# Two-bank output parts, plain transposes, one prefix sum a pair, and ScalarE's own DMA queue in a two-layer decoder trunk

## The chip, the cores and the metric

The kernel runs on one core of one Trainium2 chip. Such a core has five engines with one instruction stream each: TensorE (PE in the rows; its weight loads are PEld), VectorE (DVE), ScalarE (ACT), GpSimd (POOL) and SyncE (SP), which issues DMAs. ScalarE can issue DMAs as well. Matrix products land in PSUM, which has eight banks; everything else is held in SBUF. The metric is the device time of one execution in microseconds. A granted clock of 1.00 for TensorE means 2.4 GHz, 0.50 means 1.2 GHz.

## What is computed

The reference is a decoder of two layers over 1024 positions with a width of 1024. Layer 0 mixes positions with a gated linear recurrence (Hawk), layer 1 with a delta-rule state of 64x64 per head and 16 heads (RWKV-7). A SwiGLU feed-forward and a gated embedding product follow each. The change is inside the second mixer, whose core is this recurrence:

```python
def step(S, inp):
    r_t, w_t, k_t, v_t, a_t, b_t = inp
    sa = jnp.einsum('bhvk,bhk->bhv', S, a_t)
    S = S * w_t[:, :, None, :] + sa[..., None] * b_t[:, :, None, :] + v_t[..., None] * k_t[:, :, None, :]
    y = jnp.einsum('bhvk,bhk->bhv', S, r_t)
    return S, y
```

Around it stand projections for r, k, v, small low-rank products for the decay w, for a and for the gate g, a normalisation of k per head, and after it a normalisation of y per head, a bonus term, the gate and an output projection.

## The kernel before, in words

The 1024 positions are worked in two halves of 512, called t = 0 and 1. The width of 1024 is eight tiles of 128 rows (index j), and a tile of 128 rows holds two heads of 64. All dense products use a split of each operand into a high and a low part and three matmuls (`mm3`), with 512 columns. Their weights come by DMA in pieces of 128x512 into `raw` (two buffers while the recurrence runs), ScalarE rounds them into the high part (L239), GpSimd forms the low part (L240), and the pair stands in `whl` (four buffers). One piece serves 12 dense matmuls.

The recurrence is done in chunks of 64 positions, eight per half, by four generators in `scan()`:

- `stage1` goes over 16 pairs (half, tile). `prep` loads a, w, k and q, forms the running sum of w inside each chunk with eight scans of 64 columns (L1004), and exponentials of it. Products of these give BK and ZL; two groups of eight matmuls (`sc`) give the within-chunk products, which DVE masks out of PSUM (L1070 to L1072). A group of 16 matmuls (`bkt`, L1090) multiplies BK with a diagonal matrix `dg` of the chunk's total decays PC, which GpSimd builds (L1034); that is a transpose with scaling. ScalarE copies it out, and it is stored in DRAM (`bk`).
- `inverse` inverts the triangular matrices of two pairs at a time, with DVE work and five groups of small matmuls (w, n, u, w, v), and stores them (`inv`).
- `stage2` runs over the 16 chunks in order and carries the state SV. Per chunk: 16 matmuls `zu<-SV,ZC`, a copy to z, 16 matmuls `zu<-z,VC`, a copy to SU (ScalarE and DVE), 16 matmuls `zu<-SU,BC` whose result DVE adds to `ss` (the old state times PC, formed ahead at L1229) for the new state, and 32 matmuls into `y` (L1253, L1254): for each of 16 head slots one from SV and one from SU, accumulating in the same PSUM place. ScalarE copies y out.
- `norm2` normalises y per head and pair of tiles, with two matmuls `bsum` and two `yv` for each pair of tiles.

Which matmul follows which on TensorE is written out by a small planner. While the generators live, TensorE's instructions keep their program order (`manual_schedule`). The dense code calls `tick()` after each matmul, and a generator's next piece is put there when the planner's own clock has passed the piece's due time and when enough PSUM tiles of the ring `b` are free by its count. That ring has `BANKS` tiles; a piece that yields 2 wants two. `until()` moves the planner's clock on when no dense work is to be put in. The other engines are ordered by priorities, where `ahead(n)` moves code n places forward.

Stores of finished tiles to DRAM are issued on SP's queue, in one order with the loads of the weights. The names in the rows are those of the tiles; L116 is the helper `mm` by which all matmuls are recorded, and an fp32 matmul leaves two records in the trace.

Of the kernel before, what the change touches and what calls it, by code (L numbers as in the profile page):

```python
# [24 lines left out]

BANKS = 3
PACE = ((3, 1200), (2.5, 200))
LEAD_O, LEAD_F, LEAD_E, LEAD_P = 2, 2, 1, 2  # L30
IN = 2
# [28 lines left out]
class Kern:  # L60
# [680 lines left out]
    def rwkv_proj(self, t):  # L741
# [39 lines left out]
        def lora2(nm, bias, hs, n0, n1):  # L781
            w2 = []

            def item(n):
                if not w2:
                    w2.append(self.load_w(A["lora2_" + nm][:, n0 * 128 : n1 * 128], (n1 - n0) * 128))
                ps = self.ps("lx")
                a = (n - n0) * 128, (n - n0) * 128 + 128
                self.mm(ps, w2[0](0, *a), hs, True, False)
                self.mm(ps, w2[0](1, *a)[0:64], hs[0:64], False, True)  # L790
                self.tick()
                o = self.t2("o")
                with self.aux():
                    self.sigmoid(o, ps, self.v(bias, n), self.nb[bias][:, n : n + 1])
                nc.sync.dma_start(self.act_d[nm, n, t], o)
                self.done.add((nm, n, t))

            return [lambda n=n: item(n) for n in range(n0, n1)]
# [18 lines left out]
        def gate2(gh, gl, gs, q):  # L817
            w = []

            def item(n):  # L820
                if not w:
                    for nm in ("lora2_g", "lora2_gb"):
                        w.append(self.load_w(A[nm][:, q * 512 : q * 512 + 512], 512))
                    nc.vector.tensor_copy(w[1](0, 0, 512)[64:96], w[1](1, 0, 512)[64:96].bitcast(F32))
                a = n * 128, n * 128 + 128
                ps = self.ps("gx")
                self.mm(ps, w[0](0, *a), gh, True, False)
                self.mm(ps, w[0](0, *a), gl, False, False)
                self.mm(ps, w[0](1, *a), gh, False, False)
                self.mm(ps, w[1](0, *a)[:96], gs[:96], False, True)  # L830
                self.tick()
                o = self.t2("o")
                with self.aux():
                    nc.scalar.copy(o, ps)
                nc.sync.dma_start(self.act_d["g", 4 * q + n, t], o)
                self.done.add(("g", 4 * q + n, t))

            return [lambda n=n: item(n) for n in range(4)]
# [19 lines left out]
        def proj(i, j, nm, ext=None, xs=None, mid=None, n0=4):  # L858
            if xs is None:
                xs = self.rwkv_mix(xn, j, ext)  # L860
                self.pause(PM)

            def after(n, o, f):
                if f is not None:
                    f()
                if nm == "v":
                    ps = self.ps("vtr").rearrange("p (c k) -> p c k", c=4)
                    for c in range(4):
                        self.mm(ps[:, c, :], o[:, c * 128 : c * 128 + 128], self.cst[:, 128:256])
                    z = self.t2("vt").rearrange("p (h c k) -> p h c k", c=4, k=64)  # L870
                    with self.aux():
                        nc.scalar.copy(z, ps.rearrange("p c (h k) -> p h c k", k=64))
                    x = self.vt_d[t][:, :, :, n, :].rearrange("s h (c e) k -> e s h c k", e=2)
                    for e in range(2):
                        nc.sync.dma_start(x[e], z[e * 64 : e * 64 + 64])
                self.done.add((nm, n, t))

            for ns in self.lead([*range(KD)], LEAD_P):
                if mid is not None and n0 in ns:
                    mid()  # L880
                qs = []
                for n in ns:
                    if len(ns) > 1:
                        qs.append((self.ps("pps"), self.halves(A["rkv"][i, n], None, xs, t)))
                    else:
                        w = self.load_w(A["rkv"][i, n], 1024)
                        qs.append((self.ps("pps"), self.wx(w, KD, xs, t)))
                self.mm3(*qs)
                self.flush()
                for n, (ps, _) in zip(ns, qs):  # L890
                    o = self.t2("o")
                    with self.aux():
                        if n % 2:
                            nc.scalar.copy(o, ps)
                        else:
                            nc.vector.tensor_copy(o, ps)
                    nc.sync.dma_start(self.act_d[nm, n, t], o)
                    f = unit(n, o) if nm == "k" else None
                    self.later.append(lambda n=n, o=o, f=f: after(n, o, f))
            if not self.region:  # L900
                self.flush()
# [20 lines left out]
    def scan_begin(self, sp, pp):  # L922
        nc, A = self.nc, self.A
        self.sp, self.spp = sp, pp
        self.zu = pp.tile([128, KD, 64], F32, name="zu")
        self.yp = pp.tile([128, KD, 64], F32, name="y")
        self.Pp = sp.tile([128, NC, 65], F32, name="Pp")
        nc.vector.memset(self.Pp[:, :, 0:1], 1.0)
        self.D16 = sp.tile([128, 32, 16], F32, name="D16")
# [9 lines left out]
    def scan(self):  # L939
# [55 lines left out]
        def stage1():  # L995
            Pp = self.Pp

            def prep(t, j):
                at = ld("a", j, t)
                sw = ld("w", j, t)  # L1000
                kt = ld("k", j, t)
                L = tt("L")
                for c in range(0, TH, 64):
                    nc.vector.tensor_tensor_scan(  # L1004
                        L[:, c : c + 64], self.ones[:, 0:64], sw[:, c : c + 64], 0.0, ALU.mult, ALU.add)
                nc.scalar.activation(Pp[:, :, 1:65], c3(L), AF.Exp, scale=-C0)
                nc.scalar.activation(L, L, AF.Exp, scale=C0)
                return at, kt, L, ld("q", j, t), sw
# [2 lines left out]
            for P, (t, g, jj) in enumerate(order):  # L1011
# [17 lines left out]
                    PCs[t] = sp.tile([128, NC, KD], F32, tag="PC", name="PC", bufs=2)  # L1029
                PC = PCs[t][:, :, j]  # L1030
                nc.vector.tensor_copy(PC, Pp[:, :, 64])

                dg = sp.tile([128, NC, 64], F32, tag="dg", name="dg", bufs=1)
                nc.gpsimd.tensor_mul(dg, ident.unsqueeze(1).to_broadcast([128, NC, 64]), PC.unsqueeze(2).to_broadcast([128, NC, 64]))  # L1034

                old = (P - 3) // 2
                yield 4000, False, (lambda: old < 0 or inv[old] >= 2)
# [49 lines left out]
                pss = [c3(big("bkt", e)) for e in (500, 900)]  # L1087
                for c in range(NC):
                    for hh, me, ot in HV:
                        self.mm(pss[hh][:, c, :], BK[me, c, :, :].rearrange("p i s -> p (i s)"), dg[me, c, :])  # L1090
                        self.clock -= 77
                evac()
                evac()
                with self.ahead(AHEAD_S1):
                    for hh in range(2):
                        nc.scalar.copy(BKt[:, :, hh, :], pss[hh])
                nc.sync.dma_start(self.bk_d[t][:, :, j, :], BKt.rearrange("p c h k -> p c (h k)"))
                s1[G] += 10
                if nxt is not None:
                    yield 1000, False, None  # L1100
# [1 line left out]
        def inverse():  # L1102
# [16 lines left out]
            for G in range(NG):  # L1119
# [54 lines left out]
                with ahead():  # L1174
                    for p0 in (0, 64):
                        nc.scalar.copy(V[p0 : p0 + 32, :, :, 32:64], ps[p0 : p0 + 32].rearrange("p (j c) k -> p j c k", j=2))
                nc.sync.dma_start(self.inv_d[G // 4][:, :, 2 * (G % 4) : 2 * (G % 4) + 2, :], Vt)
                yield 1000, False, None
                inv[G] = 3

        def stage2():
# [3 lines left out]
            def state():  # L1185
                return sp.tile([128, 2, KD, 64], F32, tag="SV", name="SV", bufs=2)
# [21 lines left out]
            for t in range(2):  # L1208
# [4 lines left out]
                for c in range(NC):  # L1213
# [6 lines left out]
                    for j in range(KD):  # L1220
                        for hh, me, ot in HV:
                            self.mm(ps[me, j, :], ZL[:, j, hh * 128 : hh * 128 + 64], SV[:, hh, j, :])
                    self.clock = at + 650
                    with ahead():
                        nc.scalar.copy(z, ps)
                        if upd:
                            ss = sp.tile([128, KD, 64], F32, tag="ss", name="ss", bufs=1)
                            for hh, me, ot in HV:
                                nc.vector.tensor_mul(ss[me], SV[me, hh], PC[me, c, :].unsqueeze(2).to_broadcast([64, KD, 64]))  # L1229
                            SVn = state()  # L1230
                        if c < NC - 1:
                            nxt = load(t, c + 1, SVn)
                    yield ZLAT, False, None
                    at = self.clock
                    for j in range(KD):
# [8 lines left out]
                    if upd:  # L1244
                        for j in range(KD):
                            for hh, me, ot in HV:
                                self.mm(ps[me, j, :], BKc[:, j, hh * 64 : hh * 64 + 64], SU[:, hh, j, :])
                        with ahead():
                            for hh, me, ot in HV:
                                nc.vector.tensor_add(SVn[me, hh], ps[me], ss[me])  # L1250
                    for j in range(KD):
                        for hh, me, ot in HV:
                            self.mm(yp[me, j, :], SV[:, hh, j, :], ZL[:, j, hh * 128 + 64 : hh * 128 + 128], True, False)  # L1253
                            self.mm(yp[me, j, :], SU[me, hh, j, :], ZL[me, j, 256:320], False, True)  # L1254
                    self.clock = at + 2000
                    if c % 2 == 0:
                        ys = sp.tile([128, KD, 2, 64], F32, tag="yc", name="yc", bufs=1)
                    with ahead():
                        nc.scalar.copy(ys[:, :, c % 2, :], yp)
                    if c % 2:  # L1260
                        nc.sync.dma_start(self.y_d[t][:, :, c * 64 - 64 : c * 64 + 64], ys.rearrange("p j c k -> p j (c k)"))
                    if upd:
# [226 lines left out]
```

## Time and profile before

| | us |
|---|---|
| median of 3 runs | 3225.04 (3216.24 to 3226.09) |
| profiled execution | 3224.65 |
| its span | 3222.9 |
| PE, PEld busy | 3038.5, 2386.2 |
| DVE, ACT, POOL busy | 1618.0, 1359.2, 1301.1 |

The span runs from the first to the last instruction of the profiled execution. Busy times count an engine's instructions; a wait is put down to what came last before it ended. The kernel moves 415.20 MB by DMA, 129 GB/s on average, nearly all of it through one queue issued from SP.

### The profile page before, as it was taken

Reading aid. Unit: us, or ns where it says so; the run is one execution under the profiler, and the core shown is the slowest. Engines: PE = TensorE matmul, PEld = TensorE weight load, DVE = VectorE, ACT = ScalarE, POOL = GpSimd, SP = SyncE. Lnnn points to the kernel's source line nnn. Section 1 sums busy time; section 2 is a strip of 40 time slices with the busy share of each in tenths; the row PEclk is TensorE's granted clock in tenths of the full one; section 3 lists DMA queues with packets and bytes.
Section 4 is the critical chain, followed back from the end, with each engine's and each line's share of the span. In section 5 each row is a group of like instructions: output and inputs, shape, how many; then the busy total and the mean of one; then the engine's idle time right before and its main releaser. Section 6 shows DMA issues by size and latency. Waiting matters only on the chain. (4 is left out here: it accounts for less than half of the span.)

```text
span 3222.9 us, 45692 instructions
## 1 busy us (share of the span) xinstructions
PE 3038.5 (94%) x17160; PEld 2386.2 (74%) x17160; DVE 1618.0 (50%) x2498; ACT 1359.2 (42%) x2213; POOL 1301.1 (40%) x1082
## 2 busy tenths in 40 slices
PE   5999999999999889999999878888999999999998
PEld 4777778887867667777777556667777777888886
DVE  8765751222572467773336556688322356312145
ACT  5574742323565334334344752333322345422244
POOL 5111144444554445444223354443322345544445
PEclk9999999999999989999888998889988899999999
DMA  3111133332336464444443676544444363333323
GB/s 126 59 43 45 51 98 95 95 95 92 119 118 211 155 207 159 156 146 135 151 155 107 221 231 187 174 139 155 134 135 153 105 220 104 105 95 95 95 84 106
DMA packets 269148, 415.20 MB, mean 129 GB/s; under 512 B 40704, under 2 KB 108032, under 8 KB 266880
## 3 DMA queue, kind: packets, MB, share of 16 engines
q1 hardware_dynamic: 268640, 411.93, 39.9%
q8 instruction: 135, 2.21, 0.3%
q14 instruction: 85, 0.70, 0.1%
q10 hardware_dynamic: 288, 0.37, 0.0%
HBM read 319.92 MB, written 92.27 MB: 128 GB/s over the span
## 5 line engine op out<-in xcount | busy, mean ns | idle before, releaser
L240 POOL TENSOR_TENSOR whl<-raw,whl 128x512 fp32r<-128x512 f32 (+2 forms) x818 | 1052.4, 1292 | 1511.6 <-ACT whl L239 1458.2
L239 ACT CAST whl<-raw 128x512 fp32r<-128x512 f32 (+2 forms) x818 | 482.6, 593 | 927.2 <-PE ops L116 249.4
L116 PE MATMUL pg<-xn,whl 128*128 128x512 f32 (+1 forms) x2184 | 524.5, 394 | 7.0 <-ACT xn L290 4.8
L116 PE MATMUL ops<-hid,whl 128*128 128x512 f32 x2112 | 513.1, 400 | 19.0 <-ACT hid L290 7.2
L116 PEld LDWEIGHTS ops<-hid,whl 128*128 128x128 f32 x2112 | 400.8, 192 | 119.6 <-DVE hid L291 14.3
L116 PEld LDWEIGHTS pg<-xn,whl 128*128 128x128 f32 x2184 | 408.1, 189 | 101.9 <-ACT xn L290 6.7
L116 PE MATMUL pu<-xn,whl 128*128 128x512 f32 x1584 | 384.3, 396 | 2.4 <-ACT xn L290 1.5
L116 PEld LDWEIGHTS pu<-xn,whl 128*128 128x128 f32 x1584 | 298.9, 190 | 70.1 <-DVE xn L291 2.1
L116 PE MATMUL pps<-mix,whl 128*128 128x512 f32 x1152 | 297.6, 412 | 15.2 <-ACT mix L290 4.6
L391 DVE TENSOR_TENSOR h<-h,ops 128x512 f32<-128x512 f32 x256 | 173.7, 685 | 265.2 <-PE ops L116 264.0
L556 DVE TENSOR_TENSOR sg<-sg,pu 128x512 f32<-128x512 f32 x88 | 60.3, 685 | 445.0 <-PE pu L116 444.6
L116 PEld LDWEIGHTS pps<-mix,whl 128*128 128x128 f32 x1152 | 220.5, 194 | 82.1 <-issue 11.4
L116 PE MATMUL pg<-raw,whl 128*128 128x512 f32 x720 | 195.2, 424 | 3.3 <-ACT whl L239 2.6
L116 PEld LDWEIGHTS pg<-raw,whl 128*128 128x128 f32 x720 | 145.9, 206 | 39.6 <-ACT whl L239 3.0
L242 POOL TENSOR_SCALAR whl<-raw 128x512 fp32r<-128x512 f32 (+2 forms) x84 | 59.7, 714 | 214.3 <-PE rps L116 74.0
L116 PE MATMUL pu<-raw,whl 128*128 128x512 f32 x528 | 142.0, 420 | 2.4 <-ACT whl L239 1.8
L116 PE MATMUL rps<-xn,whl 128*128 128x512 f32 x480 | 123.2, 404 | 15.4 <-ACT xn L290 9.5
L116 PEld LDWEIGHTS pu<-raw,whl 128*128 128x128 f32 x528 | 105.7, 203 | 28.4 <-ACT whl L239 2.2
L116 PEld LDWEIGHTS rps<-xn,whl 128*128 128x128 f32 x480 | 91.9, 193 | 41.6 <-issue 11.1
L116 PE MATMUL gps<-xn,whl 128*128 128x512 f32 x480 | 117.5, 399 | 0.0
L116 PE MATMUL ops<-m,whl 128*128 128x512 f32 x480 | 114.5, 396 | 0.8 <-ACT m L290 0.8
L291 DVE TENSOR_TENSOR hid<-sg,hid 128x512 fp32r<-128x512 f32 x88 | 86.3, 980 | 49.8 <-ACT hid L290 49.7
(276 smaller groups left out, 4022.1 us busy)
## 6 DMA issues: line engine op xcount, KB each, us to landing
raw<-in_ffn_in SPq DMA_DIRECT2D x352, 256.0 KB, 2.6
raw<-in_ffn_out SPq DMA_DIRECT2D x152, 256.0 KB, 2.6
raw<-in_rkv SPq DMA_DIRECT2D x96, 256.0 KB, 3.1
zl<-ZL SPq DMA_DIRECT2D x32, 640.0 KB, 3.9
ZC<-zl SPq DMA_DIRECT2D x16, 1280.0 KB, 5.7
raw<-in_ple_gate SPq DMA_DIRECT2D x64, 256.0 KB, 2.7
raw<-in_w_in SPq DMA_DIRECT2D x48, 256.0 KB, 2.8
h<-h SPq DMA_DIRECT2D x32, 256.0 KB, 3.3
```

The lines of the kernel that those rows point to most:

```text
L116: self.nc.tensor.matmul(out, lhsT=lhsT, rhs=rhs, start=start, stop=stop)
L239: nc.scalar.copy(hl[:rows, 0, :w], raw[:rows, :w])
L240: nc.gpsimd.tensor_sub(hl[:rows, 1, :w], raw[:rows, :w], hl[:rows, 0, :w].bitcast(F32))
L242: nc.gpsimd.tensor_scalar(hl[:rows, 0, :w], raw[:rows, :w], 1.0, 0.0, ALU.mult, ALU.add)
L291: (nc.gpsimd if pool else nc.vector).tensor_sub(lo, src, hi.bitcast(F32))
L391: nc.vector.tensor_add(hs, hs, ps)
L556: nc.vector.tensor_mul(sg, sg, pu)
```

## The change

Five things change. The ring `b` has two tiles and not three (`BANKS`). `y` has two PSUM tiles, one in each of two banks: the 16 matmuls from SV go to the first, right behind `zu<-SV,ZC`; the 16 from SU go to the second, right behind `zu<-SU,BC`; ScalarE copies the first out and DVE adds the second. `bkt` is a plain transpose by TensorE with the identity, `dg` is gone, and the scaling with PC moves into the update of the state: (new product + old state) x PC, so `ss` is gone as well. One scan of 512 columns, over a mask `run` that is 0 at each chunk's start, replaces eight scans of 64. And 128 stores of tiles that ScalarE makes are issued from ScalarE.

```diff
-BANKS = 3
+BANKS = 2
...
-                nc.sync.dma_start(self.act_d[nm, n, t], o)
+                nc.scalar.dma_start(self.act_d[nm, n, t], o)
...
-                nc.sync.dma_start(self.act_d["g", 4 * q + n, t], o)
+                nc.scalar.dma_start(self.act_d["g", 4 * q + n, t], o)
...
-                        nc.sync.dma_start(x[e], z[e * 64 : e * 64 + 64])
+                        nc.scalar.dma_start(x[e], z[e * 64 : e * 64 + 64])
...
-                    nc.sync.dma_start(self.act_d[nm, n, t], o)
+                    (nc.scalar if n % 2 else nc.sync).dma_start(self.act_d[nm, n, t], o)
...
-        self.yp = pp.tile([128, KD, 64], F32, name="y")
+        self.yp = [pp.tile([128, KD, 64], F32, name=f"y{i}") for i in range(2)]
...
+            run = sp.tile([128, TH], F32, name="run")
+            nc.gpsimd.memset(run, 1.0)
+            nc.gpsimd.memset(c3(run)[:, :, 0:1], 0.0)
...
-                for c in range(0, TH, 64):
-                    nc.vector.tensor_tensor_scan(
-                        L[:, c : c + 64], self.ones[:, 0:64], sw[:, c : c + 64], 0.0, ALU.mult, ALU.add)
+                nc.vector.tensor_tensor_scan(L, run, sw, 0.0, ALU.mult, ALU.add)
...
-                dg = sp.tile([128, NC, 64], F32, tag="dg", name="dg", bufs=1)
-                nc.gpsimd.tensor_mul(dg, ident.unsqueeze(1).to_broadcast([128, NC, 64]), PC.unsqueeze(2).to_broadcast([128, NC, 64]))
...
-                        self.mm(pss[hh][:, c, :], BK[me, c, :, :].rearrange("p i s -> p (i s)"), dg[me, c, :])
-                        self.clock -= 77
+                        nc.tensor.transpose(pss[hh][:, c, :], BK[me, c, :, :].rearrange("p i s -> p (i s)"), ident[me])
+                        self.clock += 30
...
-                nc.sync.dma_start(self.bk_d[t][:, :, j, :], BKt.rearrange("p c h k -> p c (h k)"))
+                nc.scalar.dma_start(self.bk_d[t][:, :, j, :], BKt.rearrange("p c h k -> p c (h k)"))
...
-                nc.sync.dma_start(self.inv_d[G // 4][:, :, 2 * (G % 4) : 2 * (G % 4) + 2, :], Vt)
+                nc.scalar.dma_start(self.inv_d[G // 4][:, :, 2 * (G % 4) : 2 * (G % 4) + 2, :], Vt)
...
-                    self.clock = at + 650
+                    for j in range(KD):
+                        for hh, me, ot in HV:
+                            self.mm(yp[0][me, j, :], SV[:, hh, j, :], ZL[:, j, hh * 128 + 64 : hh * 128 + 128])
+                    self.clock = at + 1300
                     with ahead():
                         nc.scalar.copy(z, ps)
-                        if upd:
-                            ss = sp.tile([128, KD, 64], F32, tag="ss", name="ss", bufs=1)
-                            for hh, me, ot in HV:
-                                nc.vector.tensor_mul(ss[me], SV[me, hh], PC[me, c, :].unsqueeze(2).to_broadcast([64, KD, 64]))
-                            SVn = state()
-                        if c < NC - 1:
-                            nxt = load(t, c + 1, SVn)
+                    if upd:
+                        SVn = state()
+                    if c < NC - 1:
+                        nxt = load(t, c + 1, SVn)
...
+                            w = sp.tile([128, KD, 64], F32, tag="w", name="w", bufs=1)
                             for hh, me, ot in HV:
-                                nc.vector.tensor_add(SVn[me, hh], ps[me], ss[me])
+                                nc.vector.tensor_add(w[me], ps[me], SV[me, hh])
+                                nc.vector.tensor_mul(SVn[me, hh], w[me], PC[me, c, :].unsqueeze(2).to_broadcast([64, KD, 64]))
                     for j in range(KD):
                         for hh, me, ot in HV:
-                            self.mm(yp[me, j, :], SV[:, hh, j, :], ZL[:, j, hh * 128 + 64 : hh * 128 + 128], True, False)
-                            self.mm(yp[me, j, :], SU[me, hh, j, :], ZL[me, j, 256:320], False, True)
-                    self.clock = at + 2000
+                            self.mm(yp[1][me, j, :], SU[me, hh, j, :], ZL[me, j, 256:320])
+                    self.clock = at + 1300
...
-                        nc.scalar.copy(ys[:, :, c % 2, :], yp)
+                        nc.scalar.copy(ys[:, :, c % 2, :], yp[0])
+                        nc.vector.tensor_add(ys[:, :, c % 2, :], ys[:, :, c % 2, :], yp[1])
```

On TensorE, one chunk of `stage2` before, among dense matmuls of the feed-forward (`ops`); the last two rows stand 16 times in turn:

```order
L116 MATMUL zu<-SV,ZC 64x64 x16
L116 MATMUL ops<-hid,whl 128x512 x13
L116 MATMUL zu<-z,VC 64x64 x16
L116 MATMUL ops<-hid,whl 128x512 x13
L116 MATMUL zu<-SU,BC 64x64 x16
L116 MATMUL y<-ZC,SV 64x64
L116 MATMUL y<-ZC,SU 64x64
```

And one chunk after; `y_8222` and `y_8223` are the two tiles of y:

```order
L116 MATMUL zu<-SV,ZC 64x64 x16
L116 MATMUL y_8222<-ZC,SV 64x64 x16
L116 MATMUL ops<-hid,whl 128x512 x13
L116 MATMUL zu<-z,VC 64x64 x16
L116 MATMUL ops<-hid,whl 128x512 x3
L116 MATMUL pg<-raw,whl 128x512 x10
L116 MATMUL zu<-SU,BC 64x64 x16
L116 MATMUL y_8223<-ZC,SU 64x64 x16
L116 MATMUL pg<-raw,whl 128x512 x14
```

The SV part of y has moved in front of two runs of 13 dense matmuls, and neither part alternates with the other.

On TensorE, the end of `norm2` before, with the `yv` of its last group but one in the second row and its last `bsum` and `yv`:

```order
L116 MATMUL pg<-raw,whl 128x512 x7
L116 MATMUL yv<-v,cst 128x512 x2
L116 MATMUL pg<-raw,whl 128x512 x17
L116 MATMUL pu<-raw,whl 128x512 x24
L116 MATMUL ops<-hid,whl 128x512 x19
L116 MATMUL bsum<-b,cst 128x512 x2
L116 MATMUL ops<-hid,whl 128x512 x29
```

The same place after, again from the `yv` of the last group but one:

```order
L116 MATMUL ops<-hid,whl 128x512 x29
L116 MATMUL yv<-v,cst 128x512 x2
L116 MATMUL ops<-hid,whl 128x512 x36
L116 MATMUL bsum<-b,cst 128x512 x2
L116 MATMUL yv<-v,cst 128x512 x2
L116 MATMUL pu<-raw,whl 128x512 x24
```

60 dense matmuls stood between the two pairs, and 36 do now; the last `yv` stands right behind its `bsum`.

On ScalarE, the transposition of v in the first half after the change, with what each instruction waits for (Activation is ScalarE itself, DMAHW a DMA counter):

```order
L872 COPY vt<-vtr 128x512 [waits DMAHW1_49,PE_49]
L875 DMA vt_279<-vt 512x1x64 [waits Activation_49]
L872 COPY vt<-vtr 128x512 [waits PE_49]
L290 CAST xn<-xn 128x512 [waits DMAHW1_49]
L875 DMA vt_279<-vt 512x1x64 [waits DMAHW7_49]
L239 CAST whl<-raw 128x512 [waits PE_49,Pool_49]
```

The L875 rows stood on SP's queue before; now weight casts (L239) stand behind them. Of the 128 sends 65 name a DMA counter in such a list.

## Rows read from the trace of the kernel before

**Rows 1.** Page, busy time and share by engine, with instruction counts.

```profile
PE 3038.5 (94%) x17160; PEld 2386.2 (74%) x17160; DVE 1618.0 (50%) x2498; ACT 1359.2 (42%) x2213; POOL 1301.1 (40%) x1082
```

**Rows 2.** Stretches: length, busy PE, PEld, DVE, ACT, POOL, PEclk, DMA share, GB/s.

```profile
1523.00:1762.00 239.00, 238.05 (x1799) 182.64 (x1798) 109.17 (x147) 96.00 (x161) 67.59 (x54) 0.88 0.42 137
2318.00:2531.00 213.00, 213.00 (x1598) 163.66 (x1597) 54.90 (x76) 52.19 (x85) 47.50 (x35) 0.84 0.40 129
...
1280.00:1523.00 243.00, 232.89 (x2034) 188.32 (x2031) 159.38 (x312) 92.15 (x158) 110.86 (x84) 0.98 0.47 151
1762.00:1960.00 198.00, 169.31 (x667) 118.79 (x665) 116.56 (x162) 124.08 (x212) 90.62 (x66) 0.93 0.68 222
...
sum 1119.00, PE 1008.89 PEld 784.40 DVE 682.64 ACT 483.36 POOL 484.59; mean PE 168.15 PEld 130.73 DVE 113.77 ACT 80.56 POOL 80.76
```

**Rows 3.** Timeline of PE in one chunk: start, length, instruction, count of records.

```profile
1523.50 1.15 PE L116 MATMUL zu<-SV,ZC 128*64 128x64 f32 x32
1524.58 2.79 PE L116 MATMUL pu<-xn,whl 128*128 128x512 f32 x11
...
1527.75 1.15 PE L116 MATMUL zu<-z,VC 64*64 64x64 f32 x32
1528.83 3.25 PE L116 MATMUL pg<-xn,whl 128*128 128x512 f32 x13
...
1533.19 0.33 PE L116 MATMUL y<-ZC,SU 64*64 64x64 f32 x2
1533.45 0.33 PE L116 MATMUL y<-ZC,SV 128*64 128x64 f32 x2
...
1542.01 0.47 PE L116 MATMUL y<-ZC,SU 64*64 64x64 f32 x2
1542.41 3.88 PE L116 MATMUL pg<-xn,whl 128*128 128x512 f32 x9
```

**Rows 4.** The same two stretches, PE's instructions on y alone.

```profile
1523.00:1762.00 239.00, 76.97 (x512) 0.88 0.42 137
2318.00:2531.00 213.00, 79.93 (x512) 0.84 0.40 129
```

**Rows 5.** The stretch right behind one y group, as in rows 2.

```profile
1542.40:1546.20 3.80, 3.80 (x11) 3.03 (x11) 0.00 (x0) 0.59 (x1) 0.00 (x0) 0.56 0.68 198
```

**Rows 6.** Timeline of PE at one bkt group.

```profile
1326.96 2.00 PE L116 MATMUL bkt<-dg,BK 64*128 64x64 f32 x32
1328.89 1.43 PE L116 MATMUL pg<-xn,whl 128*128 128x512 f32 x5
```

**Rows 7.** DVE groups: shapes, count, busy us, mean ns, idle before and releaser.

```profile
L1072 DVE TENSOR_TENSOR ZL<-sc,cst 64x512 f32<-64x512 f32 x64 | 44.1, 688 | 0.9
L1004 DVE TENSOR_TENSOR_SCAN L<-ones,w 128x64 f32<-128x64 f32 x128 | 31.6, 299 | 20.2 <-DMA w<-w 13.2 <-DMA b<-r 6.2 <-DVE h L391 0.8
```

**Rows 8.** Line 482, another scan: ns min/median/max, first and last start, forms.

```profile
L482 DVE TENSOR_TENSOR_SCAN hr<-a,b x10: 1209/1216/1623, 70.9 to 375.8; 128x512 f32<-128x512 f32 x10
```

**Rows 9.** Timeline of PE in dense work alone.

```profile
2807.61 5.66 PE L116 MATMUL pu<-xn,whl 128*128 128x512 f32 x24
2813.10 5.66 PE L116 MATMUL pg<-xn,whl 128*128 128x512 f32 x24
```

**Rows 10.** Line 875, the stores of vt, as in rows 8.

```profile
L875 SPq DMA_DIRECT2D vt<-vt x32: 513/566/740, 1119.1 to 2013.9; - x32
...
DMA to landing us min/median/max: 2.3/3.3/6.1
```

**Rows 11.** PE's waits: us in total, times, longest.

```profile
PE sc L116 <- DVE ZL L1072: 16.8, 4, 6.1
PE bkt L116 <- DVE ZL L1072: 4.6, 2, 3.7
```

**Rows 12.** Timeline of PE between the last two groups of norm2.

```profile
2603.14 4.46 PE L116 MATMUL pg<-raw,whl 128*128 128x512 f32 x17
...
2618.85 1.13 PE L116 MATMUL bsum<-b,cst 128*128 128x512 f32 x2 [0.53 <-DMA b<-b]
```

## The prediction

> **What bounds the kernel now.** I read the shares of the page first, then the busy time by stretch, then TensorE's timeline inside one stretch, and last the waits. TensorE (PE) is busy 94% of the span, no other engine over 50% [rows 1], so what counts is how long its instructions take and how often it stands still. By stretches two kinds of time appear [rows 2]. From 1523 to 1762 us and from 2318 to 2531 us, the two runs of `stage2`, PE never stands still (238.05 of 239 and 213 of 213 us) but its granted clock is 0.88 and 0.84. In the six other stretches between 960 and 2318 us, whose sum is the last row, it is idle for 1119.0 - 1008.9 = 110.1 us in all. So in `stage2` a gain can come only from shorter PE work or from the clock; elsewhere also from waits.
>
> Inside a chunk of `stage2` the timeline [rows 3] shows three groups of 16 small matmuls (32 records each, since an fp32 matmul leaves two): `zu<-SV,ZC` takes 1524.58 - 1523.50 = 1.08 us and `zu<-z,VC` 1528.83 - 1527.75 = 1.08 us, both start to start. Then come 32 matmuls into `y`, which alternate between an SV operand of 128 rows and an SU operand of 64 rows. Each pair of records starts 0.26 us after the one before, 0.40 us later on, and the group ends at 1542.41. The same shapes in an unmixed group need 1.08/16 = 0.068 us a matmul; alternating they need about four times that. Counted alone, `y` holds PE for 76.97 + 79.93 = 156.9 us [rows 4]. The step from 0.26 to 0.40 us is the clock: it falls from 2.4 to 1.2 GHz while `y` runs, and is not back when the dense matmuls resume (0.56 on average over the 3.8 us after it) [rows 5].
>
> **The y parts.** The change issues the 16 SV matmuls right behind `zu<-SV,ZC` and the 16 SU ones right behind `zu<-SU,BC`, each as one group. The nearest rows are the two `zu` groups: the SV part reads the same two tiles as `zu<-SV,ZC` (operands swapped, same shapes), the SU part has the form of `zu<-z,VC`. So 16 chunks x (1.08 + 1.08) = 34.6 us in place of 156.9: **-122.3 us**. All of it is on PE, which has no idle there [rows 2], so all of it counts.
>
> **The clock behind y.** Low time in the two stretches is 2 x (0.12 x 239 + 0.16 x 213) = 125.5 us [rows 2]. At full clock `y` would take 16 x 32 x 0.26 = 133.1 us, so its excess is 23.8; one low microsecond in `y` does 0.26/0.40 = 0.65 of a full one's work, so 23.8/0.35 = 68 us of the low time lies in `y` and 57.5 in dense matmuls, which lose half of it: 28.8 us. With two separate groups of 2.1 us, each between dense matmuls, I expect no fall, since the stretch from 1280 us, which is full of single groups of 1 to 2 us such as bkt [rows 6], has a clock of 0.98 [rows 2]: **-28.8 us**. Bounds: 0 (the clock still falls) to -28.8.
>
> **bkt as transposes.** 16 groups of 16 fp32 matmuls take 1328.89 - 1326.96 = 1.93 us each [rows 6], 32 records at 60 ns. No transpose is in the trace. From above the bound is no gain; from below, one record a transpose in place of two, 0.97 us. I take the lower one, since a transpose has no two halves to add: 16 x 0.96 = **-15.4 us**, with 0 as the other end.
> The Trainium skill ("TensorE: Matmul & The Clock Gate", Terms) calls the transpose mode four times faster for FP32; by that figure the group would be an estimated 0.48 us and the term -23 us. No row here can show it.
>
> **DVE, GpSimd, ScalarE.** One scan of 512 columns (1.216 us) replaces eight of 64 (299 ns mean) [rows 7, 8]: 16 x (8 x 0.299 - 1.216) = 19 us of DVE saved; the `dg` product on GpSimd goes. `ss` and its add become `w` and a product, four 64x512 operations as before, near 0.69 us each [rows 7], but all four now follow the BC matmuls: 2.8 us against 1.4. Behind them PE has y's SU part and about 36 dense matmuls, 1.08 + 36 x 0.229 [rows 9] = 9.3 us, so this stays hidden; without that cover it costs 15 x 1.4 = 21 us. The new add into `ys` (16 x 0.7 us) has the rest of the chunk. I take 0 for all of these.
>
> **The sends.** 128 stores leave SP's queue for ScalarE's: 32 of w and a, 16 of g, 32 of vt, 24 of k, r and v, 16 of bk, 8 of inv. One of vt holds its queue for 0.57 us, the longest of them [rows 10], so up to 73 us of ScalarE, which is busy 42% [rows 1]. SP gets that back, and its weight loads are no longer behind stores that wait for ScalarE. Behind a send on ScalarE stand the weight casts (L239), for which GpSimd's subtraction and then PE wait; 65 of the 128 also wait for a DMA counter shared with SP's loads. PE's 110 us of waits there [rows 2] end on ScalarE only in part, and four `whl` buffers of 12 matmuls each cover 11 us. I take **+8 us**; bounds 0 and +73.
>
> **Two banks.** An `sc` or `bkt` group needs both banks emptied. PE waits 16.8 + 4.6 us for this now [rows 11], with mostly 12 to 24 dense matmuls between groups; the new order has mostly 23 to 29, 5.3 to 6.6 us, against three DVE operations of up to 0.69 us for each of two tiles [rows 7], about 3.5 us. I take 0, bounds -21 and +21. At the end dense work runs out: between `yv` of the last but one group and the last `bsum` stand 36 matmuls (8.2 us) and not 60, while the stores and loads between took 2618.85 - 2603.14 = 15.7 us [rows 12]; that is 7.5 us of waiting, and `yv` directly behind `bsum` some 1.5 more: **+9 us**.
>
> **Sum.** The profiled execution took 3224.65 us, 1.75 beyond its span of 3222.9; the median of the runs is 3225.04, 0.01% away. 3224.65 - 122.3 - 28.8 - 15.4 + 8 + 9 = **3075 us**.
>
> **Rivals.**
> 1. `stage2` becomes bound by its transfers. It moves 0.137 x 239 + 0.129 x 213 = 60.2 MB in 452 us [rows 2], and would have 301 us: 200 GB/s. For: the loads of 1.3 MB a chunk share the queue with weights that have two raw buffers. Against: the stretch from 1762 us moves 222 GB/s. If 180 GB/s is all, it takes 334 us, at 150 GB/s 401; the middle gives +67: 3142 us. Chance 0.10.
> 2. Two banks and the sends lengthen the waits of the other stretches: idle up by half of 110 us, 3130 us. For: `stage2`'s first half now ends later, inside the projections, where DVE and ScalarE already set the pace. Against: the wider spacing. 0.12.
> 3. The freed DVE, GpSimd and SP shorten those waits by a third: 3038 us. For: SP's stores no longer hold weights up. Against: most of those waits end on DVE work that stays. 0.08.
> 4. The transposes let the clock fall. 16 times 3.4 us at half clock cost 27 us, and the gain on bkt goes: 3075 + 27 + 15 = 3117 us. For: `y` shows that small work can lower it. Against: a bkt group is 2 us at most. 0.05. The Trainium skill (the same page, Part 4: PE-mode transpose) says that transposes do not keep the clock up as matmuls do; no run here shows it yet.
> 5. The change doesn't do what it says: `y` is slow by its own operands and not by the alternation. Then the y and clock terms go: 3226 us. Against: `zu` with the same tiles. 0.03.
> 6. Slower than before: ScalarE's sends are held until an earlier transfer lands, through the shared counters. 128 x 3.3 us [rows 10] is 422 us of ScalarE; if half reaches PE through late casts, 3075 + 211 = 3286 us. It decides from 160/128 = 1.25 us of exposed time a send. 0.02.
>
> **How the numbers follow.** The forecast has 0.60, own range 3050 to 3100 (the bkt term at 0 and half the two-bank bound above, the same bound below). 3035 to 3130 leaves out half of rivals 1 and 2, some of 3, and 5 and 6: about 0.2. Under 0.3% (10 us) a measurement of this kernel can't tell a change from none. Faster: forecast and rivals 1 to 4, 0.95. The same: rival 5, 0.03. Slower: rival 6, 0.02.
>
> **What would show it.** In the profile after: two y groups of about 1.1 us in each chunk and no row of `y` at 0.26 us a pair; granted clock near 1.0 in both `stage2` stretches, now about 165 and 140 us long; a bkt group near 1 us; a wait of some 7 us at the last `bsum`; GB/s in `stage2` near 200. I am wrong if `whl` becomes PE's releaser in `stage2` (rival 1), if the idle of the other stretches passes 150 us (rivals 2 and 6), or if the clock stays under 0.9 (rival 4).

## The result, and the profile after

The kernel after takes 3059.05 us (median of four runs, 3055.72 to 3064.93) against 3224.53 us before (four runs beside them): a ratio of 0.9494, 95% interval 0.9471 to 0.9516, or 165 us less. The prediction was 3075 us, with 3035 to 3130 as its range. The profiled execution took 3055.72 us, its span 3053.9.

Busy time by engine on the page of the kernel after, which answers to [rows 1]:

```profile
PE 2865.8 (94%) x16904; PEld 2257.6 (74%) x16904; DVE 1603.6 (53%) x2402; ACT 1355.6 (44%) x2213; POOL 1282.4 (42%) x1068
```

PE's busy time fell by 172.7 us. Its idle time was 3222.9 - 3038.5 = 184.4 us and is 3053.9 - 2865.8 = 188.1 us. So the gain is shorter PE work. The waits kept their size in sum, but not their places.

The two runs of `stage2`, from the first `zu` to the last `y`, of the kernel before (length, busy PE, PEld, DVE, ACT, POOL, granted clock, DMA share, GB/s):

```profile
1523.50:1759.10 235.60, 234.65 (x1788) 180.89 (x1788) 107.17 (x144) 93.67 (x156) 67.46 (x53) 0.88 0.42 137
2311.40:2530.60 219.20, 219.20 (x1679) 168.79 (x1679) 56.55 (x78) 55.24 (x90) 48.89 (x37) 0.85 0.39 128
```

The same two of the kernel after:

```profile
1540.60:1712.30 171.70, 164.13 (x1766) 129.48 (x1765) 116.68 (x154) 100.02 (x172) 69.59 (x52) 0.98 0.60 192
2225.50:2368.90 143.40, 143.40 (x1678) 117.46 (x1677) 60.40 (x86) 48.39 (x81) 47.95 (x36) 1.00 0.61 194
```

They were 454.8 us and are 315.1: 139.7 of the 169 us of span are here. PE executes nearly the same number of records (3467, now 3444), at a clock that is now 0.98 and 1.00. Transfers run at 192 and 194 GB/s. PE's idle time in the first run rose from 0.95 to 7.57 us. Between the two runs, where the projections of the second half stand, it fell from 73.15 to 61.71 us (before, then after):

```profile
1759.10:2311.40 552.30, 479.15 (x3361) 367.93 (x3359) 361.52 (x649) 251.37 (x435) 232.65 (x180) 0.91 0.56 178
```

```profile
1712.30:2225.50 513.20, 451.49 (x3218) 344.36 (x3216) 344.17 (x585) 236.74 (x412) 218.16 (x170) 0.94 0.59 188
```

One chunk in PE's timeline after (start, length, instruction, records), which answers to [rows 3]:

```profile
1562.59 1.15 PE L116 MATMUL zu<-SV,ZC 128*64 128x64 f32 x32
1563.57 1.10 PE L116 MATMUL y<-ZC,SV 128*64 128x64 f32 x32
1564.60 1.43 PE L116 MATMUL pg<-raw,whl 128*128 128x512 f32 x5
...
1567.78 1.15 PE L116 MATMUL zu<-z,VC 64*64 64x64 f32 x32
1568.85 3.25 PE L116 MATMUL pg<-raw,whl 128*128 128x512 f32 x13
1572.67 1.15 PE L116 MATMUL zu<-SU,BC 128*64 128x64 f32 x32 [0.58 <-DVE SU L1240]
1573.76 1.15 PE L116 MATMUL y<-ZC,SU 64*64 64x64 f32 x32
1574.84 1.42 PE L116 MATMUL pg<-raw,whl 128*128 128x512 f32 x5
```

The SV part holds PE from 1563.57 to 1564.60, 1.03 us, and the SU part from 1573.76 to 1574.84, 1.08. Over the 32 groups that is 34.6 us, start to next start; all but one take what these two take, and the SU group at 1668.52 us takes 1.90 us, at a granted clock of 0.50 and 1.4 us behind a wait of PE of 2.02 us. The bracket in the sixth row is a wait that the kernel before did not have: PE stands 0.58 us for SU.

The same view at one bkt group ([rows 6] before):

```profile
1199.86 0.71 PE L1089 MATMUL bkt<-cst,BK 64*128 64x64 f32 x16
1200.50 1.66 PE L116 MATMUL ops<-hid,whl 128*128 128x512 f32 x6
```

Sixteen records in place of 32, and 0.64 us in place of 1.93.

The end of `norm2` after ([rows 12] before):

```profile
2443.97 1.88 PE L116 MATMUL yv<-v,cst 128*128 128x512 f32 x4
2445.28 8.77 PE L116 MATMUL ops<-hid,whl 128*128 128x512 f32 x36
2453.89 1.02 PE L116 MATMUL bsum<-b,cst 128*128 128x512 f32 x2
2457.47 1.10 PE L116 MATMUL bsum<-b,cst 128*128 128x512 f32 x2 [2.56 <-DMA b<-b]
2459.41 3.61 PE L116 MATMUL yv<-v,cst 128*128 128x512 f32 x4 [0.84 <-ACT v L1288]
2463.80 5.78 PE L116 MATMUL pu<-raw,whl 128*128 128x512 f32 x24 [0.78 <-ACT v L1297]
```

And PE's longest sums of waits after (us, times, longest):

```profile
PE nps L116 <- DVE acc L302: 31.4, 8, 13.0
PE bsum L116 <- DMA b<-b: 16.1, 3, 11.8
PE sc L116 <- DVE ZL L1071: 12.0, 6, 3.6
PE rps L116 <- ACT xn L290: 10.5, 1, 10.5
PE vtr L116 <- ACT o L894: 7.2, 2, 6.1
```

Against [rows 11] the wait of sc is 12.0 us and not 16.8; that of bkt, now for the inverse's Wa, is 6.4 and not 4.6. The wait of bsum is new: it was 0.5 us in all before. Its longest, 11.8 us, stands at 1773.56 us, at the second group of the first half; at the end of `norm2` it sums to 4.4 us.

### The profile page after: what moved, and what is told of

Same layout as the page of the kernel before. It is cut to its first block, busy times and chain, and to the rows that moved or that the text cites. A ratio compares the mean times of both kernels' runs of the same rounds, so it can differ in the third digit from the quotient of the medians.

```text
span 3053.9 us, 45089 instructions
## 1 busy us (share of the span) xinstructions
PE 2865.8 (94%) x16904; PEld 2257.6 (74%) x16904; DVE 1603.6 (53%) x2402; ACT 1355.6 (44%) x2213; POOL 1282.4 (42%) x1068
## 4 chain that ended last, share of the span: by engine, by line
PE 40%; DVE 10%; DMA 7%; issue 5%; POOL 3%; ACT 3%; SPq 0%; ACTq 0%; DVEq 0%; POOLq 0%
PE pg L116 12%; PE ops L116 9%; PE pu L116 8%; PE pps L116 5%; POOL whl L240 2%; DMA zl<-ZL 2%; PE zu L116 1%; DMA raw<-in_ffn_in 1%; PE pq L116 1%; DMA raw<-in_rkv 1%; DVE ZL L1044 1%; PE y L116 1%; DVE ZL L1071 1%; ACT whl L239 1%; DMA raw<-in_w_o 1%
## 5 line engine op out<-in xcount | busy, mean ns | idle before, releaser
L239 ACT CAST whl<-raw 128x512 fp32r<-128x512 f32 (+2 forms) x818 | 482.1, 593 | 945.1 <-PE ops L116 294.6
L116 PE MATMUL ops<-hid,whl 128*128 128x512 f32 x2112 | 506.5, 396 | 10.7 <-ACT hid L290 4.9
L116 PEld LDWEIGHTS ops<-hid,whl 128*128 128x128 f32 x2112 | 394.2, 189 | 106.8 <-DVE hid L291 10.3
L116 PE MATMUL pg<-raw,whl 128*128 128x512 f32 x720 | 182.6, 403 | 7.7 <-DMA raw<-in_ffn_in 5.0
L116 PEld LDWEIGHTS pg<-raw,whl 128*128 128x128 f32 x720 | 135.6, 192 | 41.8 <-issue 6.9
L116 PE MATMUL pu<-raw,whl 128*128 128x512 f32 x528 | 133.7, 402 | 1.8 <-POOL whl L240 0.9
L116 PEld LDWEIGHTS pu<-raw,whl 128*128 128x128 f32 x528 | 98.9, 190 | 27.2 <-issue 2.4
```

The costliest lines, as they stand in the source:

```text
L116: self.nc.tensor.matmul(out, lhsT=lhsT, rhs=rhs, start=start, stop=stop)
L239: nc.scalar.copy(hl[:rows, 0, :w], raw[:rows, :w])
```

## The experiments

Microseconds "from after" below are the difference of the ratios times 3225, or the difference of medians where both kernels ran in one comparison. The kernel after was run a second time for this; its ratio is taken as 0.9488, the mean of its two (0.9494 and 0.9482). The diffs are shortened: `j, hh` stands for the loops over tiles and heads.

**Was it the alternation?** One kernel groups y in the kernel before, changing nothing else:

```diff
-for j, hh: mm(y, SV[j, hh], start); mm(y, SU[j, hh], add, stop)
+for j, hh: mm(y, SV[j, hh], start only at j == 0)
+for j, hh: mm(y, SU[j, hh], add, stop at the last j)
```

> The kernel before with one edit: the 32 y matmuls of a chunk stay in their place behind BC and in one bank, but all 16 SV ones come first and then all 16 SU ones, which add onto them. Theory (the alternation of 128-row and 64-row operands made them slow, and the clock fell with that): the y groups fall from 4.8 + 5.0 to about 1.1 + 1.1 us a chunk, the clock in the two stage2 stretches rises to about 1.0, and the time falls by 122 + 29 = 151 us, to about 3074. Rival (adding twice into the same place is what is slow, and two banks are the cure): y stays near 9.8 us a chunk and the time near 3225.

Measured: a ratio of 0.959 (0.9568 to 0.9612), 132 us less than before, where 151 were expected. The stretches of `stage2`:

```profile
1521.60:1699.40 177.80, 165.87 (x1787) 133.62 (x1786) 106.42 (x142) 89.68 (x154) 67.00 (x53) 0.98 0.56 182
2252.20:2395.90 143.70, 143.70 (x1678) 117.65 (x1677) 57.28 (x78) 54.24 (x89) 48.97 (x37) 1.00 0.60 193
```

and one chunk of it:

```profile
1551.74 1.15 PE L116 MATMUL zu<-SU,BC 128*64 128x64 f32 x32
1552.73 1.10 PE L116 MATMUL y<-ZC,SV 128*64 128x64 f32 x32
1553.76 1.15 PE L116 MATMUL y<-ZC,SU 64*64 64x64 f32 x32
1554.84 1.43 PE L116 MATMUL ops<-hid,whl 128*128 128x512 f32 x5
```

The order of 32 matmuls alone takes y from 156.9/16 = 9.8 us a chunk [rows 4] to 2.11, still adding into one bank, and the clock goes to 0.98 and 1.00. PE's busy time in `stage2` falls by 453.85 - 309.57 = 144.3 us with two records fewer than before; 11 us of that come back, since PE now waits 11.93 us in the first run and waited 0.95:

```profile
PE zu L116 <- ACT z L1225: 7.7, 3, 6.1
PE zu L116 <- DVE SU L1241: 2.2, 2, 1.4
```

The reverse: the kernel after with y back behind BC, alternating, but in two banks without any adding:

```diff
-16 x mm(y0, SV) behind zu<-SV,ZC
-16 x mm(y1, SU) behind zu<-SU,BC
+16 x (mm(y0, SV), mm(y1, SU)) behind zu<-SU,BC
```

> The kernel after with the y matmuls put back behind BC, alternating SV and SU as before, but SV into one bank and SU into the other, so that nothing is added in PSUM. Theory (alternation): y is slow again, 0.26 us a pair of records and more, the clock falls behind it, and the time rises by about 151 us over after, to about 3210. Rival (the second write into the same place was slow): y stays at 2.2 us a chunk and the time near 3060.

Measured: 3200.29 us, 0.9922 (0.9905 to 0.9938), 140 us more than after. Its y in the timeline, with the step within the group, and the stretches:

```profile
1558.95 0.33 PE L116 MATMUL y<-ZC,SU 64*64 64x64 f32 x2
1559.21 0.33 PE L116 MATMUL y<-ZC,SV 128*64 128x64 f32 x2
...
1560.23 0.47 PE L116 MATMUL y<-ZC,SV 128*64 128x64 f32 x2
1560.64 0.47 PE L116 MATMUL y<-ZC,SU 64*64 64x64 f32 x2
```

```profile
1546.20:1782.30 236.10, 233.07 (x1766) 177.26 (x1766) 115.61 (x156) 102.25 (x173) 67.57 (x52) 0.87 0.43 142
2295.50:2513.20 217.70, 217.70 (x1679) 167.88 (x1679) 59.95 (x86) 48.82 (x81) 48.32 (x36) 0.86 0.40 129
```

The steps of 0.26 and 0.40 us are back, and so is the low clock, with nothing added in PSUM. In the kernel before, the y group at 1533 us [rows 3] starts at a granted clock of 1.00 and ends at 0.50 (PE on y alone: length, busy PE, clock, DMA share, GB/s):

```profile
1533.00:1538.50 5.50, 5.50 (x44) 1.00 0.50 147
1539.00:1542.40 3.40, 3.40 (x18) 0.50 0.00 0
```

The two runs together show that the alternation is the cause, and that neither the adding nor the banks are. What in it costs, the change between 128 and 64 rows or that between the two operands, was not tried. A change of place alone does not: the matmuls of the SU group go in turn to the lower and the upper 64 rows, and take 1.08/16 = 0.068 us each.

**The sends.** All 128 stores back on SP's queue, in after:

```diff
-nc.scalar.dma_start(self.act_d[nm, n, t], o)
+nc.sync.dma_start(self.act_d[nm, n, t], o)
```

(and so at L835, L875, L897, L1096 and L1176)

> The kernel after with all 128 moved stores back on SP's queue. Theory (the sends cost almost nothing, and freed SP gives almost nothing): 3055 to 3070. The prediction's term of +8 us says 8 us less than after, about 3051. Rival (SP's stores hold weight loads up, and moving them is worth time): over 3075.

Measured: 3069.88 us, 0.9516 (0.9500 to 0.9532), about 9 us more than after. That is inside the theory's range for the time, but on the other side of the predicted term. The intervals of after (0.9471 to 0.9516, and 0.9463 to 0.9502 the second time) overlap this one, so that the gain from moving the sends rests on medians; but the term, by which this run should be 8 us faster than after, would put it at a ratio of 0.9463, which lies outside its interval. The trace doesn't show a place for the gain: PE's idle time is 3068.2 - 2870.8 = 197.4 us, but the second trace of after itself has 3068.4 - 2869.3 = 199.1. What the traces do show is a price on the other side: PE's waits that end on ScalarE's weight casts (L239) sum to 14.8 and 22.0 us in the two traces of after, and to 7.4 us here.

**bkt.** The transposes as fp32 matmuls by the identity, in PE's same order:

```diff
-nc.tensor.transpose(pss[hh][:, c, :], BK, ident)
+nc.tensor.matmul(pss[hh][:, c, :], lhsT=BK, rhs=ident)
```

> The kernel after with bkt's 16 plain transposes made as fp32 matmuls by the identity, in the same order. Theory (each is two records again, 1.93 us a group where the transposes took 0.64, all of it on PE's path): 16 x 1.29 = 20.6 us more than after, about 3080. Rival (the spacing of groups around it hides it, since PE waits there anyway): under 10 us more.

Measured: 3068.25 us, 0.9511 (0.9496 to 0.9526), about 7 us more than after. The rival is right. The line of bkt, after first and then here (busy us, mean ns, idle before it):

```profile
L1089 PE MATMUL bkt<-cst,BK 64*128 64x64 f32 x256 | 13.0, 234 | 6.7 <-DVE Wa L1149 6.4 <-DVE ZL L1071 0.4
```

```profile
L1089 PE MATMUL bkt<-cst,BK 64*128 64x64 f32 x512 | 35.4, 284 | 7.2 <-DVE Wa L1149 7.2
```

The groups are back at 1.93 us (x32 records from 1196.34 to 1198.27), and this line has 22 us more, yet the time only 7. PE's busy time is 2880.8 - 2865.8 = 15 us higher and its idle time 3062.9 - 2880.8 = 182.1, 6 us lower than in the trace of after. A second trace of after (below) has 11 us more idle time than the first, so this difference alone proves little. The two stretches that hold the bkt groups, from 940 us to the first `zu` and between the runs of `stage2`, tell more (after, then here):

```profile
940.00:1540.60 600.60, 564.19 (x3723) 438.72 (x3721) 335.19 (x573) 257.81 (x439) 272.87 (x212) 0.95 0.52 166
```

```profile
940.00:1546.90 606.90, 575.55 (x3859) 452.00 (x3857) 339.97 (x573) 259.87 (x442) 275.00 (x212) 0.95 0.51 164
1717.70:2232.50 514.80, 456.86 (x3346) 353.37 (x3344) 345.97 (x585) 236.63 (x412) 217.97 (x170) 0.94 0.58 188
```

PE's idle time in the two is 31.35 + 57.94 = 89.3 us here and 92.2 us with three parts undone (below), the two runs with matmuls. In the runs with transposes and the same order on PE it is 98.1 and 104.7 (after, twice), 107.6 (sends on SP), 109.0 (eight scans) and 104.3 (one bank, order kept). So the longer groups do take up time in which PE would otherwise wait. The granted clock of the whole span is 0.969 to 0.972 in the nine executions of after, and 0.969 to 0.974 in the four with matmuls.

**The scan.** Eight scans of 64 columns a pair in after:

```diff
-nc.vector.tensor_tensor_scan(L, run, sw, 0.0, mult, add)
+for c in range(0, TH, 64): tensor_tensor_scan(L[c:c+64], ones, sw[c:c+64], 0.0, mult, add)
```

> The kernel after with the prefix sum of a pair made again as eight scans of 64 columns in place of one of 512. Theory (VectorE has room, as the prediction took: its term was 0): the 19 us more of VectorE's work move the time by less than 5 us from after. Rival (PE's waits for VectorE in the projections, 31 us for nps<-acc and 12 for sc<-ZL in the trace after, stand behind it): 10 to 19 us more, about 3070 to 3078.

Measured: 3073.2 us, 0.9521 (0.9503 to 0.9538). The kernel after in the same comparison:

> The kernel after, unchanged, beside the three others on the same chip: 3059, ratio 0.949. It is there to tell differences of 5 to 10 us from differences between the chips.

took 3062.77 us (3056.44 to 3070.18), 0.9482 (0.9463 to 0.9502). So the eight scans cost 10 us: the rival's size. VectorE's busy time is 1622.5 us here and 1603.6 and 1606.9 in the two traces of after, 16 to 19 us less, of which some 10 reach the end.

**All three undone together**, with y as in after:

> The kernel after with three parts undone together: the 128 stores back on SP's queue, the bkt transposes as fp32 matmuls by the identity, eight scans a pair. y stays in its two groups and two banks. Theory (the three small parts add up; undone alone they cost 8, 8 and 10 us): 26 us more than after, 3087, close to the 0.959 of e1_one_bank, which has only the y part. Rival (they stand behind the same waits, so that one hides the others): 8 to 15 us more, 3069 to 3076.

Measured: 3084.38 us, 0.9561 (0.9548 to 0.9574), 24 us more than after, and clear of both its intervals. The three add up. Grouping y alone gave 0.959, so after is 33 us faster than that; 24 of these are the three parts, and some 9 us, about the size of the intervals, have no place.

**Banks and order.** y in one bank, with its early SV part, and three banks for the big tiles:

```diff
-BANKS = 2
+BANKS = 3
-mm(yp[0], SV); mm(yp[1], SU); ys = copy(yp[0]) + yp[1]
+mm(yp, SV, start at j == 0); mm(yp, SU, add); ys = copy(yp)
```

> The kernel after with y in one bank (16 SV matmuls in their new early place, 16 SU matmuls that add onto them behind BC), so no second tile and no add on VectorE, and the bank that comes free given back to the big tiles (three banks). Theory (two banks cost PE some waits, 12.0 us for sc<-ZL and 6.4 for bkt<-Wa in the trace after; the prediction took 0 with bounds of 21 us): 10 to 20 us less than after, 3039 to 3049. Rival (those waits end on VectorE's ZL and Wa themselves, not on a bank): within 5 us of after.

Measured: 3071.72 us, 0.9515 (0.9495 to 0.9534): 9 us more than after in the same comparison, where the theory wanted 10 to 20 less and the rival no more than 5 either way. The same with the planner's pace lowered:

> The same as e6_y_one_bank, with the planner's pace lowered from 3 and 2.5 to 2.6 and 2.1, so that the recurrent work is spread over fewer dense matmuls, and more of these are left for the end of norm2. Theory (norm2's end stands still for lack of dense work: 6 us in the trace after, from 2369 to 2457.5 us): 5 to 10 us less than e6_y_one_bank. Rival (the closer spacing lengthens the waits for VectorE in stage1 by more than that): as much or more than e6_y_one_bank.

Measured: 3090.61 us, 0.9571 (0.9550 to 0.9591), 19 us more than its neighbour. And one bank for y, but two for the big tiles, so that PE's order is that of after:

> The kernel after with y in one bank, added there, without the add on VectorE, and still two banks for the big tiles, so that PE's order is that of after. Theory (the loss of e6_y_one_bank came from the order that three banks make): within 5 us of after, 3056 to 3066. Rival (early y matmuls held in one bank cost it): about 3070, as e6_y_one_bank.

Measured: 3059.27 us, 0.9484 (0.9471 to 0.9497): the same as after. So the second y bank, the add on VectorE, and one or two places in PSUM are worth nothing either way. Three banks for the big tiles lose some 9 us, by medians in intervals that overlap. They come with another order of work from the planner, which is the likely cause; three banks in the order of after were not run, and which rows cost the time was not traced.

**The pace**, in after, first half 3 to 3.2, or second half 2.5 to 2.3:

> The kernel after with the planner's pace for the first half raised from 3 to 3.2. Theory (closer spacing cost e7_slower_pace 19 us in stage1, so wider spacing gives some back): 5 to 10 us less than after, about 3053. Rival (the second half then runs out of dense work at the end of norm2): as much or more than after.

> The kernel after with the planner's pace for the second half lowered from 2.5 to 2.3, so that norm2 ends with dense work left. Theory (its end stands still for 6 us of 89 in the trace after): up to 6 us less, about 3055. Rival (closer spacing costs more in the recurrent parts before): 5 to 10 us more, about 3068.

Measured: 3066.57 us, 0.9507 (0.9491 to 0.9523), and 3055.74 us (3046.43 to 3062.83), 0.9466 (0.9446 to 0.9487). By medians the first loses some 6 us where its theory wanted a gain, and the second is the lowest of all, some 7 us less than after; neither can be told from after by its interval, so no version is shown to beat it.

## Why the prediction was right, point by point

The sum was 3224.65 - 149.5. The span fell by 169.0 us: PE's busy time by 172.7, where the three PE terms said 166.5, and its idle time rose by 3.7, where the other two said 17. The forecast lies 19 us above the profiled execution; 6 of them are in the PE terms and 13 in those two. The mechanism that carries the sum, y and its clock, was right. That the rest came so near is in part luck: the gain on bkt was put 8 us too high, those on the scan and the sends together some 27 us too low, and these misses partly cancel.

- **y, -122.3.** Measured 34.6 us for the 32 groups, which is the figure forecast; to the tenth by chance, since 16 x (1.03 + 1.08) is 33.8 and one slow group makes up the rest. The nearest rows, `zu` with the same tiles, were the right price, and the two experiments on the order confirm the reason; the rival that y is slow by its own operands is out.
- **The clock behind y, -28.8.** The direction and place were right: 0.98 and 1.00 in `stage2`. The kernel before with y grouped gives the size: 144.3 us of PE's time in `stage2`, of which 156.9 - 34.95 = 121.95 are busy time of y, so 22.4 for the rest. The term was 6 us too large, and 3.6 of these are low time that is left: the clock of 0.98 over 177.8 us means 7.1 us at the lower level, which lose half.
- **bkt, -15.4.** Mis-sized twice. The group takes 0.64 us and not 0.97, so PE spends 16 x 1.29 = 20.6 us less on it; the end moves by about 7 us only. The step that failed is pricing every microsecond of PE as one of the span: in these stretches PE also waits, and with longer groups it waits 9 to 15 us less (89.3 against 98.1 and 104.7). The Trainium skill ("TensorE: Matmul & The Clock Gate", Terms) has FP32 transposes four times faster; the trace gives 1.93/0.64 = 3.0, between that and my factor of two.
- **Rival 4, the transposes lower the clock.** Out: 0.969 to 0.972 with them, 0.969 to 0.974 without. The stretch from 940 us to the first `zu`, with half the bkt groups, has 0.95 after and 0.94 before. The price of 3.4 us a group was given without its source; the low time behind one y group is 2 x (1 - 0.56) x 3.8 = 3.3 us [rows 5]. The Trainium skill (the same page, Part 4: PE-mode transpose) says that transposes do not keep the clock up; between dense matmuls, in groups of 0.64 us, no run here shows a loss.
- **DVE at 0.** Wrong by some 10 us in the scan's part: "the cover" that I named was that of `stage2`, while the scans stand in stage1, where VectorE sets part of the pace (sc and bkt wait for it: 12.0 and 6.4 us above; of the 31.4 us of nps 13.0 stand there). The step that failed is pricing 19 us of VectorE at nothing in the stretch whose waits end on VectorE. For the four products behind BC 0 was nearly right: the next chunk's `zu<-SV,ZC` never waits for them (0.0 us), and the waits for SU are 3.8 us in the first run of `stage2` and none in the second.
- **Sends, +8.** The sign failed: undoing them costs about 9 us by medians and does not gain 8. I priced the time that a send holds ScalarE, and wrote "SP gets that back" without a figure; the bound went to 0 and not below. That is the step that failed. A send does hold ScalarE for what was read in [rows 10]; line 875 after has

```profile
L875 ACTq DMA_DIRECT2D vt<-vt x32: 515/516/1167, 1120.5 to 1931.7; - x32
```

  and among ScalarE's waits (us, times, longest) stands

```profile
ACT whl L239 <- DMA vt<-vt: 15.1, 4, 5.0
```

  that is, four casts that start only when a vt store has landed. Busy times leave out the issuing of DMAs, so ScalarE's (1355.6 us, before 1359.2) says nothing of it. PE felt the sends: its waits for casts are 12.2 to 22.0 us in the five traces with PE's order of after and the sends on ScalarE, and 7.4 and 5.7 in the two with the sends on SP. So a price of the size of the term's 8 us is there. What outweighs it is what SP gets back, which was put at nothing; where that arises stays open. Rival 6 is out: the time is 3059 us and not 3286.
- **Two banks, 0.** Right within its bounds: the waits of sc and bkt for VectorE sum to 12.0 + 6.4 + 0.4 = 18.8 us against 21.4 [rows 11], and three banks were not faster. The run with one bank for y and the order kept says nothing of these two; it shows that y's second bank is free.
- **The end of norm2, +9.** About right: that stretch has 88.6 - 82.56 = 6.0 us of idle PE and had 0.5, and behind it stand the 0.84 and 0.78 us in the rows above. The wait sits at the bsum that was named, at 2.56 us and not 7.5; others of the same stretch make up part of the difference. Not forecast was the wait of 11.8 us for `b` in the first half, which no term has. Two banks do not make it, for with three of them, and y in one, bsum waits 17.7 us in all; nor does grouping y, which alone leaves it at 0.5. Its cause stays open.
- **Rival 1, transfers.** 192 and 194 GB/s, against the 200 forecast; in the first run of `stage2` PE's 7.6 us of idle time have 1.6 for `whl`, in the second there are none. Out.
- **Rivals 2 and 3, more or fewer waits.** PE's idle time stayed in sum (184.4 and 188.1 us), and the second trace of after has 199.1; the two rivals' differences of 55 and 37 us are excluded. Each has a part that came true: 11.4 us less between the runs of `stage2`, and new waits in the first run and for `b`.

Set beside one another, the parts as undone one by one (y and its clock 140, scan 10, sends 9, bkt 7) come to 166 us, and the whole is 165. The agreement is closer than the terms are known: y grouped alone in the kernel before gave 132, and the intervals of the small parts are as wide as the parts.

## What to carry to other kernels

Small matmuls of different shapes belong in groups of one shape: look in the timeline for a step between starts that is several times that of the same shape alone, and price the grouping by that row. A microsecond saved on the bounding engine counts whole only where that engine has no idle time; in a stretch with waits it was worth a third here (7 of 20.6 us). In such a stretch time saved on the engine on which the waits end counts too (10 of 16 to 19 us here), so a term for it should not be put at 0. And when work moves from one queue to another, price both sides: what the new queue loses and what the old one gains.

## What was not expected of the hardware

- A plain transpose of 64x128 fp32 came at 0.64/16 = 40 ns in a group, one record each.
- Alternating matmuls start 0.26 us apart at a clock of 2.4 GHz, in one bank or in two, where 1.03/16 = 0.064 us is the step in a group of one shape; and the clock falls to its lower level within the alternating group, while the same 32 matmuls in groups leave it at 0.98 to 1.00.
- Two traces of one kernel differ by 11 us in PE's idle time (188.1 and 199.1), so a wait of that size is found by medians and not by one trace.
